# Input projection of a hybrid decoder layer in another order of groups and feature tiles, with fewer adaLN steps to a chunk

## The chip, the cores and the metric

One core of a Trainium2 chip (trn2) runs the whole layer in one launch. The metric is the device time of one execution in microseconds; three runs of the kernel before are shown, and one further execution was profiled.

## What is computed

One layer over 256 tokens of 2048 features, batch 1, all in float32:

```python
mod = silu(c) @ W_ada + b_ada                    # 2048 x 12288
shift1, scale1, gate1, shift2, scale2, gate2 = split(mod)
u = x*(1+scale1) + shift1
proj = u @ w_in                                  # 2048 x 9216: GLU 2x1024 | q | k | v | gate logits 2x2048
A = silu(LN(conv31(a_lin * sigmoid(a_gate)))) @ w_conv_out + b_conv_out
B = causal_attention(rope(q), rope(k), v) @ w_attn_out
x = LN(alpha*x + (1+gate1) * ((sigmoid(g_A)*A + sigmoid(g_B)*B) @ w_out))
u = x*(1+scale2) + shift2
x = LN(alpha*x + (1+gate2) * ((silu(conv3(a)) * val) @ w_down))     # [a | val] = u @ w_up
```

## The kernel before

Activations lie feature-major: a tile of 128 features by 256 tokens. A weight **chunk** is 128 rows by 1024 columns, 512 KB. `chunk` (L380) loads it into one of five `raw` buffers by a DMA from SP's queue, ScalarE rounds it to `wh` (L393), and VectorE takes the remainder `wl` (L394); `wh` and `wl` have three buffers each. TensorE then does wh x uh, wh x ul and wl x uh for eight blocks of 128 columns (`feat`, L401, 24 matmuls a chunk), or 12 matmuls of 512 columns for v (`toks`, L409). `uh` and `ul` are the rounded activation and its remainder.

`group` (L419) runs a row of chunks for 1024 output columns into four PSUM banks. The projection w_in has nine groups g of 1024 columns (0 and 1 the GLU input, 2 q, 3 k, 4 v, 5 to 8 the gate logits) and 16 feature tiles k, 144 chunks in all. An item (g, k0, k1) of `in_item` (L477) runs group g over feature tiles k0 to k1; a first item of a group is copied out of PSUM by ScalarE (L487), a later one is added by VectorE (L485). The list `items` (L656) sets the order.

adaLN's product with W_ada is no matmul: VectorE adds up 16 scaled row tiles for each **piece** of 1024 columns (L207; the first rows L199, L201), each from a 512 KB transfer `araw` on SP's queue, into the same `raw` buffers as the weights. A finished piece is transposed by TensorE (`pa`, L223), summed by VectorE (`red`, L225) or ScalarE (L229), and added to b_ada (`mod`, L234 and L236); `make_u` (L245) then makes `u` (L254), `uh` (L242) and `ul` (L243). The first two pieces give two feature tiles each, the next three give four each, and then come gate1, shift2 and scale2, gate2.

Three queues of background work are stepped from `chunk`: `ada_q` by rates["ada"] per chunk (a step is charged 1.15), `att_q` (rope, L576, and the attention heads) by 0.7, and `bg_q` by rates["bg"]. Into `bg_q` goes `conv` (L514), branch A's 31 taps over pairs of channel tiles: ScalarE scales a shifted tile into one of two `pr` buffers (L533) and VectorE adds it (L535, 512 columns), every sixth tap is a pair of fused operations on VectorE (L531). `conv_norm` (L538) follows: the mean by matmuls with ones (`pm`, L542) and L544, the subtraction L551, squares L552, variance `pv` (L554), L557, L558, L560, L566, silu L568 and the rounding to `chi` (L242). conv of half g starts when group g (0 or 1) is complete. w_attn_out (16 chunks) follows the projection, then w_conv_out (16), which needs `chi`, then w_out (32), w_up and w_down.

Each engine runs its instructions in one list, in order. That list isn't the order of the code: a scheduler places every instruction by an estimate of its own when the program is built.

Of the kernel before, what the change touches and what calls it, by code (L numbers as in the profile page):

```python
# [17 lines left out]
KT = D // 128  # L18
# [15 lines left out]
def layer_kernel(ctx: ExitStack, tc: tile.TileContext, x, c, w_ada, b_ada, w_in, conv_dw_w, conv_dw_b,  # L34
# [3 lines left out]
    x = x[0]  # L38
    w_ada, b_ada, w_in, w_conv_out, w_attn_out, w_out, w_up, w_down = (
        t[0] for t in (w_ada, b_ada, w_in, w_conv_out, w_attn_out, w_out, w_up, w_down))  # L40
# [12 lines left out]
    def slot(i, shape, dt, name):  # L53
        return big.tile(shape, dt, tag=f"h{i}", name=name)
# [22 lines left out]
    def wide(i, dt, name):  # L77
        return [slot(i + j, [128, 8, 256], dt, f"{name}{j}") for j in range(2)]

# [1 line left out]
    ident = cst.tile([128, 128], F32, name="ident")  # L81
    rows = slot(13, [128, 6, 128], F32, "rows")
    nc.scalar.dma_start(rows[0:16, 0], c.rearrange("o (r p) -> (o r) p", p=128))
# [49 lines left out]
        put(ropec, k_rope[0])  # L133
        put(ropes, k_rope[1])

# [1 line left out]
    xT = wide(0, F32, "xT")  # L137

    def turn_x(a, b, late=False):
# [15 lines left out]
        i = k * FT + t  # L155
        return fw[i // 88][:, i % 88:i % 88 + 1]

# [1 line left out]
    mod = cst.tile([128, 96], F32, name="mod")  # L159

    ada_done = [0]
# [214 lines left out]
    rates = {"ada": 0.0, "bg": 0.0, "att": 0.7}  # L376
    r_ada, r_bg, r_att = Rate(), Rate(), Rate()

# [1 line left out]
    def chunk(src, width, two=False):  # L380
        n = src.shape[0] // 128
        raw = st.tile([128, 1024], F32, tag="raw", name="wraw")[:, :n * width]
        if n > 1:
            nc.sync.dma_start(raw.rearrange("p (j c) -> p j c", j=n), src.rearrange("(j p) c -> p j c", j=n))
        elif two:
            nc.sync.dma_start(raw.rearrange("p (a b) -> p a b", a=2), src)
        else:
            nc.sync.dma_start(raw, src)
        if not quiet[0]:
            tick()  # L390
        wh = st.tile([128, 1024], F32R, tag="wh", name="wh", bufs=3)[:, :n * width]
        wl = st.tile([128, 1024], F32R, tag="wl", name="wl", bufs=3)[:, :n * width]
        nc.scalar.copy(wh, raw)  # L393
        nc.vector.tensor_tensor(wl, raw, wh.bitcast(F32), OP.subtract)  # L394
        if ada_done[0] < cap[0] and not quiet[0]:
            r_ada.step(ada_q, rates["ada"])
        r_att.step(att_q, rates["att"])
        r_bg.step(bg_q, rates["bg"])
        return wh, wl
# [40 lines left out]
            held = []  # L440
        return banks

# [1 line left out]
    lin = slot(6, [128, 8, 256], F32, "lin")  # L444
    gat = slot(7, [128, 8, 256], F32, "gat")
    qk = [slot(8, [128, 8, 256], F32, "q"), slot(9, [128, 8, 256], F32, "k")]
# [59 lines left out]
            elif g == 4:  # L506
                att_q.append(attention())

# [1 line left out]
    cacc, chi = [None], []  # L510

    pr = wk.tile([128, 2, 2, 256], F32, name="pr", bufs=1)
# [57 lines left out]
        yield 5.6  # L570
        quiet[0] = False

# [1 line left out]
    rps = []  # L574

    def rope(i):  # L576
# [19 lines left out]
    def attention():  # L596
# [50 lines left out]
        for i in range(4):  # L647
            cs = slice(i * 512, (i + 1) * 512)
            nc.vector.tensor_copy(flat(oh[1])[:, cs], flat(q)[:, cs])

# [1 line left out]
    ra0 = 1.0  # L652
    G0 = 4
    ra, rb = 0.35, 1.5
    items = [(g, 0, 2, 1.0, 0.0) for g in range(G0)] + [(g, 2, 4, ra0, 0.0) for g in range(G0)]
    items += [(g, 0, 4, ra0, 0.0) for g in range(G0, 9)]  # L656
    items += [(0, 4, 8, ra0, 0.0), (1, 4, 8, ra0, 0.0), (2, 4, 12, ra0, 0.0), (3, 4, 12, ra0, 0.0),
              (0, 8, KT, ra0, 0.0), (1, 8, KT, ra, rb), (2, 12, KT, ra, rb), (3, 12, KT, ra, rb)]
    items += [(g, 4, KT, ra, rb) for g in range(4, 9)]

    for _ in range(8):
        next(ada_q[0])
# [114 lines left out]
            ada_until(NB)  # L777
            drain(bg_q)

# [1 line left out]
    def norm(k, n, center):  # L781
        o = xT[k // 8][:, k % 8:k % 8 + n]
        op = nc.vector.tensor_tensor(o, o, (lc if center else la)[:, None, :].to_broadcast([128, n, 256]),
                                     OP.subtract if center else OP.mult)
        if k >= 2:
            idle(op)
# [31 lines left out]
    rest = norm_rest()  # L818
    bg_q.append(rest)

# [1 line left out]
    NP = 7  # L822
    free = [2, 3, 4, 5, 6, 7, 9, 11, 16]
    pslots, hslots = free[:NP], free[NP:] + free[:NP] + [0, 1]
# [45 lines left out]
        rates["bg"] = 0.3  # L870
    drain(bg_q)

# [1 line left out]
    lrows = [slot(i, [128, D], F32, n) for i, n in ((14, "l2g"), (15, "l2b"))]  # L874
    for r, src in zip(lrows, (ln2_g, ln2_b)):
        nc.gpsimd.dma_start(r, bass.AP(tensor=src.tensor, offset=src.offset, ap=[[0, 128], [1, D]]))
# [105 lines left out]
```

## Time and profile before

| what | value |
|---|---|
| median of three runs | 1479.33 us (1477.72 to 1479.35) |
| span of the profiled execution | 1477.4 us; its own time as a run isn't given apart |
| TensorE (PE) busy | 1417.7 us, 96% |
| VectorE (DVE) busy | 1108.8 us, 75% |
| ScalarE (ACT) busy | 796.9 us, 54% |
| DMA | 358.53 MB, mean 243 GB/s |

The span runs from the first to the last instruction; the median of the runs is 1.9 us above it. PEld is the load of a matmul's weights, which overlaps PE. A busy TensorE may still run at the lower granted clock or stand at a matmul whose end is only modelled, so busy time is read together with the count of matmuls.

### The profile page before, as it was taken

Reading aid. Unit: us, or ns where it says so; the run is one execution under the profiler, and the core shown is the slowest. Engines: PE = TensorE matmul, PEld = TensorE weight load, DVE = VectorE, ACT = ScalarE, POOL = GpSimd, SP = SyncE. Lnnn points to the kernel's source line nnn. Section 1 sums busy time; section 2 is a strip of 40 time slices with the busy share of each in tenths; the row PEclk is TensorE's granted clock in tenths of the full one; section 3 lists DMA queues with packets and bytes.
Section 4 is the critical chain, followed back from the end, with each engine's and each line's share of the span. In section 5 each row is a group of like instructions: output and inputs, shape, how many; then the busy total and the mean of one; then the engine's idle time right before and its main releaser. Section 6 shows DMA issues by size and latency. Waiting matters only on the chain.

```text
span 1477.4 us, 26835 instructions
## 1 busy us (share of the span) xinstructions
PE 1417.7 (96%) x10691; PEld 1364.2 (92%) x10691; DVE 1108.8 (75%) x1398; ACT 796.9 (54%) x1250; POOL 27.7 (2%) x57
## 2 busy tenths in 40 slices
PE   4899999999999989998999999999999999999996
PEld 4889999989999989997999999999999998888886
DVE  6788888998989879896877767988765545446456
ACT  3546436669987655345545576555444444343342
POOL 2000000210000000000000000000000000000000
PEclk9999999999999999999999999999999999999998
DMA  9999899886567657987799977778776676655662
GB/s 310 328 302 334 299 339 310 256 280 209 175 194 222 210 173 254 310 297 226 242 307 315 323 248 218 240 246 254 238 217 183 180 224 215 193 172 173 189 202 100
DMA packets 154990, 358.53 MB, mean 243 GB/s; under 512 B 12172, under 2 KB 26466, under 8 KB 154608
## 3 DMA queue, kind: packets, MB, share of 16 engines
q1 hardware_dynamic: 152704, 352.37, 74.0%
q0 software_dynamic: 1872, 4.33, 0.9%
q8 instruction: 83, 1.36, 0.4%
q14 instruction: 43, 0.35, 0.1%
q10 hardware_dynamic: 288, 0.12, 0.0%
HBM read 353.10 MB, written 2.10 MB: 240 GB/s over the span
## 4 chain that ended last, share of the span: by engine, by line
PE 75%; DMA 13%; DVE 8%; issue 2%; ACT 2%; SPq 0%; DVEq 0%; ACTq 0%
DMA araw<-in_w_ada_dram 9%; PE acc0a L405 5%; PE acc0a L407 5%; PE acc0a L406 5%; PE acc1a L405 5%; PE acc1a L407 5%; PE acc1a L406 5%; PE acc2a L406 3%; PE acc2a L407 3%; PE acc2a L405 3%; PE acc3a L405 3%; PE acc3a L406 3%; PE acc3a L407 3%; DVE wl L394 3%; DVE acc L207 2%
## 5 line engine op out<-in xcount | busy, mean ns | idle before, releaser
L393 ACT CAST wh<-wraw 128x1024 fp32r<-128x1024 f32 (+1 forms) x483 | 496.7, 1030 | 559.5 <-PE acc3a L416 132.7
L394 DVE TENSOR_TENSOR wl<-wraw,wh 128x1024 fp32r<-128x1024 f32 (+1 forms) x483 | 577.1, 1198 | 252.1 <-ACT wh L393 248.1
L207 DVE SCALAR_TENSOR_TENSOR acc<-araw,ccol,acc 128x1024 f32<-128x1024 f32 (+1 forms) x182 | 225.4, 1238 | 84.3 <-DMA araw<-in_w_ada_dram 82.6
L405 PE MATMUL acc0a<-u2h,wh 128*128 128x256 f32 x352 | 99.3, 282 | 4.8 <-ACT u2h L325 4.8
L407 PE MATMUL acc0a<-u2h,wl 128*128 128x256 f32 x352 | 100.3, 285 | 3.1 <-DVE wl L394 3.1
L405 PE MATMUL acc1a<-u2h,wh 128*128 128x256 f32 x352 | 99.4, 283 | 0.0
L406 PE MATMUL acc0a<-u2l,wh 128*128 128x256 f32 x352 | 99.4, 282 | 0.0
L406 PE MATMUL acc1a<-u2l,wh 128*128 128x256 f32 x352 | 99.2, 282 | 0.0
L407 PE MATMUL acc1a<-u2h,wl 128*128 128x256 f32 x352 | 99.2, 282 | 0.0
L533 ACT ACTIVATE pr<-hc,cw 128x256 f32<-128x256 f32 x200 | 88.8, 500 | 11.7 <-DVE cacc L535 11.3
L405 PE MATMUL acc0a<-uh,wh 128*128 128x256 f32 x256 | 74.9, 292 | 7.1 <-ACT uh L242 7.1
L407 PE MATMUL acc0a<-uh,wl 128*128 128x256 f32 x256 | 74.5, 291 | 3.2 <-DVE wl L394 3.2
L406 PE MATMUL acc0a<-ul,wh 128*128 128x256 f32 x256 | 73.4, 287 | 1.6 <-DVE ul L243 1.6
L405 PE MATMUL acc2a<-uh,wh 128*128 128x256 f32 x256 | 73.1, 286 | 0.5 <-ACT gb L487 0.5
L406 PE MATMUL acc2a<-ul,wh 128*128 128x256 f32 x256 | 73.4, 287 | 0.0
L405 PE MATMUL acc1a<-uh,wh 128*128 128x256 f32 x256 | 73.3, 286 | 0.0
L407 PE MATMUL acc1a<-uh,wl 128*128 128x256 f32 x256 | 73.2, 286 | 0.0
L407 PE MATMUL acc2a<-uh,wl 128*128 128x256 f32 x256 | 73.2, 286 | 0.0
L406 PE MATMUL acc1a<-ul,wh 128*128 128x256 f32 x256 | 73.2, 286 | 0.0
L405 PE MATMUL acc3a<-uh,wh 128*128 128x256 f32 x256 | 73.2, 286 | 0.0
L407 PE MATMUL acc3a<-uh,wl 128*128 128x256 f32 x256 | 73.0, 285 | 0.0
L406 PE MATMUL acc3a<-ul,wh 128*128 128x256 f32 x256 | 72.9, 285 | 0.0
(438 smaller groups left out, 4349.8 us busy)
## 6 DMA issues: line engine op xcount, KB each, us to landing
araw<-in_w_ada_dram SPq DMA_DIRECT2D x176, 512.0 KB, 5.1
wraw<-in_w_up_dram SPq DMA_DIRECT2D x176, 512.0 KB, 4.8
wraw<-in_w_in_dram SPq DMA_DIRECT2D x144, 512.0 KB, 4.9
wraw<-in_w_down_dram SPq DMA_DIRECT2D x55, 512.0 KB, 4.5
wraw<-in_w_down_dram SPq DMA_DIRECT2D x44, 384.0 KB, 3.7
wraw<-in_w_out_dram SPq DMA_DIRECT2D x32, 512.0 KB, 5.5
araw<-in_w_ada_dram SPq DMA_DIRECT2D x32, 256.0 KB, 5.7
wraw<-in_w_attn_out_dram SPq DMA_DIRECT2D x16, 512.0 KB, 4.5
```

Of the source, the lines that this page charges most:

```text
L207: op = nc.vector.scalar_tensor_tensor(acc, r, ccol[:, k:k + 1], acc, OP.mult, OP.add)
L393: nc.scalar.copy(wh, raw)
L394: nc.vector.tensor_tensor(wl, raw, wh.bitcast(F32), OP.subtract)
L405: nc.tensor.matmul(o, wh[:, cs], ah, start=first and i % 2 == 0, stop=False, skip_group_check=True)
L406: nc.tensor.matmul(o, wh[:, cs], al, start=False, stop=False, skip_group_check=True)
L407: nc.tensor.matmul(o, wl[:, cs], ah, start=False, stop=last, skip_group_check=True)
L533: nc.scalar.activation(pr[:, k % 2, i], src, AF.Copy, scale=w)
```

## The change

The table of items is replaced. Items (g, 0, 2) and (g, 2, 4) are now taken for five groups and not four; then four groups get tiles 4 to 8 and three groups tiles 4 to 12 ahead of the first complete group; 30 items stand where 26 stood. The rate of adaLN steps in the early items is 0.95 for the first five and 0.85 after, where it was 1.0; in the late items it is 0.42, where it was 0.35. Comment lines are emptied as well.

```diff
-    ra0 = 1.0
-    G0 = 4
-    ra, rb = 0.35, 1.5
-    items = [(g, 0, 2, 1.0, 0.0) for g in range(G0)] + [(g, 2, 4, ra0, 0.0) for g in range(G0)]
-    items += [(g, 0, 4, ra0, 0.0) for g in range(G0, 9)]
-    items += [(0, 4, 8, ra0, 0.0), (1, 4, 8, ra0, 0.0), (2, 4, 12, ra0, 0.0), (3, 4, 12, ra0, 0.0),
-              (0, 8, KT, ra0, 0.0), (1, 8, KT, ra, rb), (2, 12, KT, ra, rb), (3, 12, KT, ra, rb)]
-    items += [(g, 4, KT, ra, rb) for g in range(4, 9)]
+    ra, rb = 0.42, 1.5
+    early = [(g, 0, 2) for g in range(5)] + [(g, 2, 4) for g in range(5)] + [(g, 0, 4) for g in range(5, 9)]
+    early += [(g, 4, 8) for g in range(4)] + [(g, 4, 12) for g in range(4, 7)] + [(0, 8, KT)]
+    late = [(g, 8, KT) for g in range(1, 4)] + [(g, 12, KT) for g in range(4, 7)] + [(7, 4, KT), (8, 4, KT)]
+    items = [(*it, 0.95 if i < 5 else 0.85, 0.0) for i, it in enumerate(early)] + [(*it, ra, rb) for it in late]
```

On SP's list, counted from its start in transfers of 512 KB, adaLN stands before and now at: 15 and 14 after the eighth chunk of w_in, 41 and 37 after the 36th, 70 and 61 after the 68th, 90 and 92 after the 144th, 99 and 101 after w_conv_out, 128 and 128 after w_out; 192 and 192 at the end. The lines below the table move up by three, so L706 is now L703.

The third piece of adaLN (feature tiles 4 to 7), on TensorE's list. `pa` are the transposes of its sums, uh_94 the rounded tiles 0 to 7. Before, within the 26th chunk of the projection:

```order
L405 MATMUL acc3a<-uh_94,wh 128x256
L406 MATMUL acc3a<-ul_96,wh 128x256
L223 MATMUL pa<-ident,acc 128x128 x8
L407 MATMUL acc0a<-uh_94,wl 128x256
L405 MATMUL acc0a<-uh_94,wh 128x256
```

Now, behind the 36th chunk and ahead of the first chunk on tile 4:

```order
L405 MATMUL acc3a<-uh_94,wh 128x256
L406 MATMUL acc3a<-ul_96,wh 128x256
L407 MATMUL acc3a<-uh_94,wl 128x256
L223 MATMUL pa<-ident,acc 128x128 x4
L405 MATMUL acc0a<-uh_94,wh 128x256
L405 MATMUL acc1a<-uh_94,wh 128x256
```

The transposes stood ten chunks ahead of the first use of the new tiles, and now the second half of them stands directly ahead of it. VectorE's list behind them reads, now:

```order
L225 TENSOR_REDUCE red<-pa 128x4
L394 TENSOR_TENSOR wl<-wraw,wh 128x1024
L236 SCALAR_TENSOR_TENSOR mod<-red,bada 128x4
L207 SCALAR_TENSOR_TENSOR acc<-araw,ccol,acc 128x1024
L243 TENSOR_TENSOR ul_96<-u,uh_94 128x256 x4
```

A wl now stands between the reduction and the sum in mod.

The end of w_attn_out, on VectorE's list. cacc is the conv's sum, gb the gate of branch B, L706 (now L703) its product with the banks of w_attn_out's second group. Before:

```order
L551 TENSOR_TENSOR cacc<-cacc,pr 128x1024 x2
L394 TENSOR_TENSOR wl<-wraw,wh 128x1024
L207 SCALAR_TENSOR_TENSOR acc<-araw,ccol,acc 128x1024
L706 TENSOR_TENSOR gb_1379<-acc0a,gb_1379 128x512
L394 TENSOR_TENSOR wl<-wraw,wh 128x1024
L706 TENSOR_TENSOR gb_1379<-acc1a,gb_1379 128x512
L557 TENSOR_SCALAR pr<-pv 128x256
L706 TENSOR_TENSOR gb_1379<-acc2a,gb_1379 128x512
L560 RECIPROCAL pr<-pr 128x256
L706 TENSOR_TENSOR gb_1379<-acc3a,gb_1379 128x512
L394 TENSOR_TENSOR wl<-wraw,wh 128x1024
L566 TENSOR_TENSOR cacc<-cacc,pr 128x256 x2
```

Now:

```order
L703 TENSOR_TENSOR gb_1355<-acc3a,gb_1355 128x512
L207 SCALAR_TENSOR_TENSOR acc<-araw,ccol,acc 128x1024
L394 TENSOR_TENSOR wl<-wraw,wh 128x1024
L535 TENSOR_TENSOR cacc<-cacc,pr 128x512 x5
L531 SCALAR_TENSOR_TENSOR cacc<-hc,cw_1382,cacc 128x256 x2
L535 TENSOR_TENSOR cacc<-cacc,pr 128x512 x5
L531 SCALAR_TENSOR_TENSOR cacc<-hc,cw_1382,cacc 128x256 x2
L535 TENSOR_TENSOR cacc<-cacc,pr 128x512 x5
L531 SCALAR_TENSOR_TENSOR cacc<-hc,cw_1382,cacc 128x256 x2
L551 TENSOR_TENSOR cacc<-cacc,pr 128x1024 x2
L557 TENSOR_SCALAR pr<-pv 128x256
L560 RECIPROCAL pr<-pr 128x256
```

In both, the last wl shown is that of w_conv_out's third chunk. Fifteen tap adds and three pairs of L531 stood ahead of w_attn_out's last chunks and now stand behind that wl. On ScalarE's list the same holds of 26 instructions of L533, which now stand between the wh of that chunk and L544; behind them come five L229 ahead of L558, and no L393 until chi is made. On TensorE's list, now, with ohi the rounded attention output:

```order
L406 MATMUL acc3a<-olo,wh 128x256
L407 MATMUL acc3a<-ohi,wl 128x256
L542 MATMUL pm<-cacc,ones 128x256 x2
L554 MATMUL pv<-sq,ones 128x256 x4
L223 MATMUL pa<-ident,acc 128x128 x4
L554 MATMUL pv<-sq,ones 128x256 x4
L223 MATMUL pa<-ident,acc 128x128 x4
L405 MATMUL acc0a<-chi,wh 128x256
```

The last pm and all pv stood ahead of the last w_attn_out matmuls and now stand behind them; the eight pa stood some ten chunks later.

## Rows read from the trace of the kernel before

**Rows 1.** The page: span, and part 1 (busy time, share, instructions).
```profile
span 1477.4 us, 26835 instructions
...
PE 1417.7 (96%) x10691; PEld 1364.2 (92%) x10691; DVE 1108.8 (75%) x1398; ACT 796.9 (54%) x1250; POOL 27.7 (2%) x57
```

**Rows 2.** Waits of TensorE, 20 to 240 us: us in total, times, longest.
```profile
PE acc0a L405 <- ACT uh L242: 7.1, 3, 4.6
PE acc0a L407 <- DVE wl L394: 3.2, 4, 2.2
PE acc0a L406 <- DVE ul L243: 1.6, 1, 1.6
```

**Rows 3.** Windows: width, PE busy (matmuls), granted clock, DMA share, GB/s.
```profile
45.00:50.00 5.00, 5.00 (x44) 1.00 0.90 307
...
55.00:60.00 5.00, 4.56 (x21) 0.50 1.04 348
60.00:65.00 5.00, 5.00 (x40) 0.91 0.96 346
...
95.00:100.00 5.00, 2.78 (x22) 1.00 0.91 321
```

**Rows 4.** Timeline of TensorE about 50 us: start, us, what, idle before and releaser.
```profile
50.23 0.60 PE L223 MATMUL pa<-ident,acc 128*128 128x128 f32 x4
55.44 0.58 PE L405 MATMUL acc0a<-uh,wh 128*128 128x256 f32 x1 [4.62 <-ACT uh L242]
```

**Rows 5.** Timelines of VectorE and ScalarE in the same stretch.
```profile
51.36 0.68 DVE L225 TENSOR_REDUCE red<-pa 128x4 f32<-128x512 f32 x1
...
53.99 1.10 ACT L254 ACTIVATE u<-xT,mod 128x256 f32<-128x256 f32 x2
```

**Rows 6.** Window of all engines: PE, PEld, DVE, ACT, POOL busy, clock, DMA.
```profile
230.00:480.00 250.00, 250.00 (x1928) 243.04 (x1927) 231.16 (x332) 199.12 (x376) 15.66 (x32) 1.00 0.74 233
```

**Rows 7.** Timeline of TensorE about the end of w_attn_out.
```profile
525.68 1.24 PE L554 MATMUL pv<-sq,ones 128*128 128x256 f32 x5
...
527.59 0.28 PE L406 MATMUL acc3a<-olo,wh 128*128 128x256 f32 x1
527.71 0.28 PE L407 MATMUL acc3a<-ohi,wl 128*128 128x256 f32 x1
533.26 0.58 PE L405 MATMUL acc0a<-chi,wh 128*128 128x256 f32 x1 [5.27 <-ACT chi L242]
```

**Rows 8.** Groups by line and form: busy us, mean ns, idle before and releasers.
```profile
L394 DVE TENSOR_TENSOR wl<-wraw,wh 128x1024 fp32r<-128x1024 f32 x439 | 535.0, 1223 | 206.9 <-ACT wh L393 203.0 <-PE pg L889 1.5 <-PE acc3a L407 0.9
L207 DVE SCALAR_TENSOR_TENSOR acc<-araw,ccol,acc 128x1024 f32<-128x1024 f32 x167 | 214.2, 1282 | 82.4 <-DMA araw<-in_w_ada_dram 81.1 <-ACT acc L205 0.3 <-DVE wl L394 0.2
...
L229 ACT ACTIVATE junk<-pa 128x128 f32<-128x128 f32 x48 | 13.3, 276 | 4.1 <-PE pa L223 3.1
L229 ACT ACTIVATION_READ_ACCUMULATOR junk<-pa 128x1 f32 x48 | 9.4, 196 | 0.0
```

**Rows 9.** Timeline of ScalarE, 492 to 528 us.
```profile
492.90 1.71 ACT L533 ACTIVATE pr<-hc,cw 128x256 f32<-128x256 f32 x4
...
517.16 0.38 ACT L544 ACTIVATE pr<-pm 128x256 f32<-128x256 f32 x1 [1.13 <-PE pm L542]
...
519.67 2.04 ACT L552 ACTIVATE sq<-cacc 128x1024 f32<-128x1024 f32 x2
...
522.70 1.28 ACT L555 ACT_TABLE_LOAD   x1
...
527.55 0.42 ACT L558 ACTIVATE pr<-pr 128x256 f32<-128x256 f32 x1 [3.36 <-DVE pr L557]
```

**Rows 10.** Timeline of VectorE, 415 to 417 us.
```profile
415.03 0.87 DVE L531 SCALAR_TENSOR_TENSOR cacc<-hc,cw,cacc 128x256 f32<-128x256 f32 x2
...
416.15 1.41 DVE L535 TENSOR_TENSOR cacc<-cacc,pr 128x512 f32<-128x512 f32 x2
```

**Rows 11.** Waits of TensorE, 620 to 800 us.
```profile
PE acc0a L405 <- ACT wh L393: 2.0, 1, 2.0
```

## The prediction

> **What bounds the kernel now.** Read the page first: TensorE is busy 96% of the span [rows 1], so only its idle time and its slow clock can change the time; the question at each place is who lets it go last. The waits of TensorE over the first 240 us come next [rows 2]: 7.1 us for uh, the rounded activations, 4.6 of them in one piece; 3.2 us for wl, the weight remainders; 1.6 us for ul. Then the windows [rows 3]. At 55 to 60 us, just behind the long wait, the granted clock is 0.50, the lower of the two levels (1.2 of 2.4 GHz), and 21 matmuls ran; at 60 to 65 us 40 ran, where a full window holds 44. So the clock cost (23+4)/44 of 5 us, 3.1 us, of which 0.44 was still the wait: 2.6 us. At 95 to 100 us there is a wait of 2.2 us and the clock stays at 1.00. The DMA share there is 0.91 to 1.04 at 321 to 348 GB/s: the DMA engines are full, so a 512 KB tile costs 0.524 MB / 346 GB/s, about 1.5 us. The timeline shows what the long wait is made of [rows 4, 5]: TensorE ends its ready chunks and turns adaLN's sums at 50.23, VectorE reduces them at 51.36, ScalarE makes u at 53.99, and the next matmul starts at 55.44.
>
> From 230 to 480 us TensorE is busy all the time while VectorE is busy 231 of 250 us [rows 6]: the conv of branch A is hidden there, with little room. The next idle time is at the end of w_attn_out [rows 7]: the last matmul starts at 527.71, the first of w_conv_out at 533.26, a wait of 5.3 us for chi, the normalized conv.
>
> **The change part by part.** I count in weight chunks: 1 to 144 are w_in, 145 to 160 w_attn_out. One is 24 matmuls that start 0.12 us apart [rows 7], 2.9 us.
>
> *Opening, transfers.* Between chunks 8 and 36 SP's list has 26 adaLN transfers before and 23 now. A chunk with its share of adaLN takes (1 + 26/28) x 1.5 = 2.9 us of DMA before, TensorE's own pace, and 2.7 us now. So DMA stops being the last at these chunks. The waits behind the long one, 2.5 us for uh, 1.6 us for ul and 3.2 us for wl [rows 2], should mostly go: the fourth and fifth adaLN piece stand 4 or more chunks ahead of their use on TensorE's list, and I take half of the wl waits as gone: -5.7 us.
>
> The Trainium skill (DMA: Bandwidth & Descriptors, section Bandwidth; HBM Reference) has a core that streams alone at about 425 GB/s, so the DMA engines would have had room before and those 5.7 us would stay: 1502 in place of the forecast below. Here the share stands at 0.96 to 1.04 with 346 to 348 GB/s [rows 3], so I go by the rows.
>
> *Opening, the long wait.* Ten chunks now run before the second piece is needed, not eight, and TensorE turns its sums before the last of them. One chunk, 2.9 us, lies under the chain of 5.2 us from the turning to the first matmul [rows 4]: 2.3 us of wait are left, about the one at 97 us that kept the clock. That is 4.6 + 2.6 - 2.3 = -4.9 us. But the third piece, which before was turned ten chunks ahead of its use, is now turned directly ahead of it: TensorE's list goes from that transpose to matmuls on the new tiles. Behind it come the reduction (0.68), one wl (1.22), the add to mod, four u of 0.55 and the cast: as long as the chain of 5.2 us [rows 5, 8]. So the wait and the slow clock come again, chunk 37 in place of chunk 9: +7.2 us. Opening in all: -3.4 us. Ends: -11 if the new wait stays hidden, +2 if DMA stays last.
>
> *Middle.* The items go from 26 to 30, so 16 more adds of 512 columns on VectorE, some 11 us, and g0's projection ends at chunk 84 and not 68, so the same conv has 76 chunks and no longer 92 to hide under. VectorE had 19 us in 250 free [rows 6]; buffers of three chunks take up local excess. I charge +1 us, ends 0 and +4.
>
> *The conv's tail.* This decides. VectorE's list holds, behind the wl of w_conv_out's third chunk, 15 tap adds and 3 pairs of L531; ScalarE's holds 26 scalings behind the wh of that chunk; before, none stood there. That wh is the third ahead of TensorE and there are three buffers, so it waits for the one that TensorE frees with its last w_attn_out matmul. Both lists run in order, so all that stands behind it runs while TensorE has nothing. Worked out from that last matmul:
> - the last product with gb (about 0.7), one adaLN step (1.28) and wl (1.22) [rows 8]: 3.0 us with overlap (2.5 to 3.2);
> - the taps: two adds take 1.41 and a pair of L531 0.87 [rows 10], so VectorE alone needs 15 x 0.70 + 3 x 0.87 = 13.1 us; ScalarE needs 13 x 0.86 = 11.1 us (four scalings in 1.71 [rows 9]). They alternate over two buffers, so a little more than the longer: 14.0 (11.4 to 16);
> - from the mean to the first chi matmul: the stretch L544 to the end of L552 was 4.6 us, table load and probe 1.5, L558 to the matmul 5.7 [rows 7, 9], and ScalarE now has five adaLN sums before L558, 5 x 0.47 = 2.4 [rows 8]: 14.2. Weight copies stood inside these before and do not now: 12.0, with 0.5 for the pm matmuls (11 to 14.7).
>
> Together 29.5 us against 5.3: +24.2. TensorE's own 10 pm and pv matmuls (five of these take 1.24 [rows 7]) and 8 transposes now lie inside the wait: -3.1. The slow clock behind the wait is paid in both. Net **+21 us** (16.5 to 25.5).
>
> *w_out.* Before its last group the program asks for nine pieces at once: ten transfers in a row before, eight now, 3.0 us of DMA less. TensorE waited 2.0 us there [rows 11]: -2 us (0 to -4, if a slow clock behind the wait goes with it).
>
> The sum is 21 - 3.4 - 2 + 1 = +16.6 on the profiled execution's span of 1477.4 [rows 1]: 1494.0. The median of the runs stands 1.9 us above that span, so I forecast **1496 us**.
>
> **The rivals.**
> 1. *The opening is starved and recovers whole, and the tail is cheap: faster.* All the waits of rows 2 (11.9) and the 2.6 of clock go, w_out gives 4, taps run at VectorE's start spacing of 0.60 (15 x 0.60 + 2.6 = 11.6), the copies take 2.5 and the chain 9: 23.1 - 5.3 - 3.1 = 14.7 against 18.5, so 1475.5. It decides if the tail costs under 15.5 us net. For it: the full DMA engines. Against it: the third piece's transpose stands directly before its use. 0.06. The Trainium skill (Perfetto Trace Analysis, section Identifying the Most-Contended Engine) would lean this way, as the change feeds the engine with the highest occupancy; by its section Optimization Strategy, which wants regimes with different bounds interleaved, the conv's shorter cover speaks against it.
> 2. *The opening recovers whole, the tail as forecast*: -14.5 + 21 - 2 + 1, some 1485. 0.09; its lower part falls within no change.
> 3. *The change does not do what it says*: adaLN's transfers are 192 in both, only later, and if it was the chain and not DMA that held the opening, nothing is won there: 1501. 0.10.
> 4. *VectorE becomes the bound of the last 76 chunks*: 11 us of adds on 19 us of room, met by conv that is pressed into fewer chunks; 8 us more, 1504. For it: rows 6. Against it: adaLN's steps per chunk also move. 0.13.
>
> **How the numbers follow.** The forecast has 0.62. Range 1485 to 1507: it takes in rivals 2 to 4 and most of the tail's bounds, and leaves out rival 1 and sums of several bounds. About 0.2%, 3 us, is what a measurement of this kernel can tell from no change. Faster 0.06 (rival 1), the same 0.04 (the lower part of rival 2), slower 0.90.
>
> **What would show it.** Right: a TensorE wait for chi of 27 to 32 us, with a row of L533 and L535 and no weight copies in it; a wait of some 5 us at chunk 37 with a clock of 0.50 behind it; a wait below 3 us at chunk 11; less than 2 us before w_out's last group. Wrong: a chi wait below 20 us, or VectorE's waits (wl) of more than 3 us in all between 230 and 500 us. The forecast fails if the conv's taps are found done before w_attn_out ends.

## The result, and the profile after

The change is slower by much more than forecast: a median of 1533.18 us (1531.39 to 1536.65, four runs) beside 1479.34 us for the kernel before on the same chip, a ratio of 1.0365 with an interval of 1.0346 to 1.0383. The forecast was 1496 us, with a range that ended at 1507. The sign was right, the size was not: +54 us in place of +17.

The page of the changed kernel, span and part 1, against [rows 1]:

```profile
span 1530.9 us, 26858 instructions
...
PE 1431.3 (93%) x10691; PEld 1370.1 (89%) x10691; DVE 1119.4 (73%) x1414; ACT 800.9 (52%) x1252; POOL 27.5 (2%) x57
```

The same 10691 matmuls stand in it. TensorE is busy 13.6 us longer and idle 39.9 us longer. To see where, I take from TensorE's timeline the start of the first matmul of each stage, and subtract:

| stage on TensorE (us) | before | after | difference |
|---|---|---|---|
| start to the first w_attn_out matmul | 477.5 | 492.9 | +15.4 |
| w_attn_out, to its last matmul | 50.2 | 46.8 | -3.4 |
| from there to the first chi matmul | 5.5 | 36.2 | +30.6 |
| w_conv_out, to the first w_out matmul | 49.6 | 49.0 | -0.5 |
| w_out, to the first u2 matmul | 119.4 | 122.2 | +2.8 |
| w_up, to the first w_down matmul | 514.4 | 523.0 | +8.6 |
| first w_down matmul to the end of the span | 260.7 | 260.7 | 0 |

Half of the loss is the conv's tail (30.6 - 3.4 = 27.2 of 53.5). The projection, forecast at -2.4 us (opening and middle), lost 15.4, and w_up, which no term of the sum named, 8.6.

*Projection.* Waits of TensorE after, first 20 to 160 us (against [rows 2]), then 160 to 492 us:

```profile
PE acc0a L405 <- ACT uh L242: 13.0, 3, 7.1
PE acc0a L406 <- DVE ul L243: 1.0, 1, 1.0
```

```profile
PE s L604 <- DMA k<-rp: 2.3, 1, 2.3
PE acc0a L405 <- ACT wh L393: 2.2, 2, 1.9
PE acc0a L407 <- DVE wl L394: 1.6, 3, 0.7
PE acc2a L415 <- DVE k L485: 0.8, 1, 0.8
PE tp L624 <- ACT pp L619: 0.8, 1, 0.8
PE acc0a L417 <- DVE wl L394: 0.7, 1, 0.7
PE acc0a L415 <- ACT wh L393: 0.7, 1, 0.7
PE acc2a L405 <- DVE lin L485: 0.5, 1, 0.5
```

Windows after, with the columns of [rows 3] after the engines' (PE, PEld, DVE, ACT, POOL, then clock, DMA share, GB/s):

```profile
55.00:60.00 5.00, 1.29 (x7) 0.66 (x5) 1.96 (x2) 5.00 (x10) 0.00 (x0) 0.99 1.05 399
60.00:65.00 5.00, 4.07 (x19) 4.07 (x20) 4.52 (x6) 1.47 (x2) 0.00 (x0) 0.50 0.99 306
...
95.00:100.00 5.00, 5.00 (x44) 5.00 (x43) 4.47 (x6) 1.05 (x1) 0.00 (x0) 1.00 0.96 332
...
145.00:150.00 5.00, 0.79 (x3) 0.79 (x4) 3.85 (x7) 3.21 (x8) 0.00 (x0) 0.52 0.92 307
150.00:155.00 5.00, 5.00 (x37) 5.00 (x35) 1.90 (x3) 0.11 (x2) 0.00 (x0) 0.79 0.68 207
```

The longest wait, 7.1 us, is the one at chunk 37, with the low clock in it and behind it (0.52 and 3 matmuls from 145 to 150 us, 37 matmuls in the next 5 us where a full window holds 44). The long wait of before did not shrink: it is at chunk 11 now (3.7 us for uh and 1.0 us for ul), and the clock falls to 0.50 again. Of the waits of before the small ones for wl are gone. From 160 us on a handful of waits of 0.5 to 2.3 us, 9.6 us in all, stands where the kernel before had 2.2 us, the 1.6 us for ul of [rows 2] the longest.

What the chain ahead of chunk 11 is made of, on TensorE and ScalarE (against [rows 4, 5]):

```profile
52.18 0.60 PE L223 MATMUL pa<-ident,acc 128*128 128x128 f32 x4
59.22 0.39 PE L405 MATMUL acc0a<-uh,wh 128*128 128x256 f32 x1 [3.67 <-ACT uh L242]
```

```profile
55.38 1.09 ACT L254 ACTIVATE u<-xT,mod 128x256 f32<-128x256 f32 x2
58.74 0.73 ACT L242 CAST uh<-u 128x256 fp32r<-128x256 f32 x2
```

From the turning to the first matmul it takes 7.0 us now, before 5.2. Between u and uh ScalarE's list has three copies out of v's banks (L487) and the rounding of a weight chunk (L393); u itself stands behind the first of those copies, which waits for TensorE.

The window of [rows 6] after: VectorE has 32 us free, more than the 19 before. Under it the group of [rows 8] that changed most, L207, whose idle time before it rose from 82.4 to 111.8 us.

```profile
230.00:480.00 250.00, 242.11 (x1920) 236.49 (x1919) 217.91 (x303) 171.03 (x306) 15.70 (x32) 0.99 0.76 245
```

```profile
L207 DVE SCALAR_TENSOR_TENSOR acc<-araw,ccol,acc 128x1024 f32<-128x1024 f32 x167 | 214.3, 1283 | 111.8 <-DMA araw<-in_w_ada_dram 109.6 <-ACT acc L205 1.6
```

*Tail.* TensorE about the end of w_attn_out, against [rows 7]; then VectorE; then ScalarE; then all engines in three windows:

```profile
539.71 0.28 PE L407 MATMUL acc3a<-ohi,wl 128*128 128x256 f32 x1
559.88 2.08 PE L542 MATMUL pm<-cacc,ones 128*128 128x256 f32 x4 [19.88 <-DVE cacc L531]
564.77 3.78 PE L554 MATMUL pv<-sq,ones 128*128 128x256 f32 x8 [2.82 <-ACT sq L552]
...
568.86 1.89 PE L554 MATMUL pv<-sq,ones 128*128 128x256 f32 x8
...
575.91 0.58 PE L405 MATMUL acc0a<-chi,wh 128*128 128x256 f32 x1 [4.58 <-ACT chi L242]
```

```profile
542.80 1.28 DVE L207 SCALAR_TENSOR_TENSOR acc<-araw,ccol,acc 128x1024 f32<-128x1024 f32 x1
543.99 1.23 DVE L394 TENSOR_TENSOR wl<-wraw,wh 128x1024 fp32r<-128x1024 f32 x1
545.13 1.42 DVE L535 TENSOR_TENSOR cacc<-cacc,pr 128x512 f32<-128x512 f32 x2
546.85 1.49 DVE L535 TENSOR_TENSOR cacc<-cacc,pr 128x512 f32<-128x512 f32 x2 [0.31 <-ACT pr L533]
...
559.34 0.88 DVE L531 SCALAR_TENSOR_TENSOR cacc<-hc,cw,cacc 128x256 f32<-128x256 f32 x2
562.40 2.36 DVE L551 TENSOR_TENSOR cacc<-cacc,pr 128x1024 f32<-128x1024 f32 x2 [2.19 <-ACT pr L544]
570.79 0.42 DVE L557 TENSOR_SCALAR pr<-pv 128x256 f32<-128x256 f32 x1 [6.03 <-PE pv L554]
```

```profile
561.99 0.38 ACT L544 ACTIVATE pr<-pm 128x256 f32<-128x256 f32 x1 [3.41 <-PE pm L542]
563.66 2.19 ACT L552 ACTIVATE sq<-cacc 128x1024 f32<-128x1024 f32 x2 [1.29 <-DVE cacc L551]
565.87 1.28 ACT L555 ACT_TABLE_LOAD   x1
```

```profile
550.00:575.00 25.00, 8.64 (x28) 6.20 (x28) 14.44 (x23) 15.89 (x42) 0.00 (x0) 0.63 0.00 0
559.00:568.00 9.00, 5.30 (x12) 3.78 (x13) 3.54 (x5) 3.98 (x5) 0.00 (x0) 0.50 0.00 0
570.00:572.00 2.00, 1.34 (x8) 0.75 (x6) 0.42 (x1) 1.16 (x7) 0.00 (x0) 1.00 0.00 0
```

The chain reads as forecast, link by link: the last copies to 545.1, the row of L533 and L535 to 560.2 with no weight copy in it, then mean, variance and chi. What is new to the eye is the clock: its mean of 0.63 over the gap is 0.50 up to 568 us and 1.00 from 570 us. All pm and the first half of pv run at 0.50: a record takes 0.52 us (2.08 for 4) and 0.47 us (3.78 for 8). The second half of pv takes 0.24 us a record (1.89 for 8), as before, where five took 1.24 us [rows 7].

### The profile page after: what moved, and what is told of

The parts are those of the page before. It is cut to its first block, busy times and chain, and to the rows that moved or that the text cites. A ratio compares the mean times of both kernels' runs of the same rounds, so it can differ in the third digit from the quotient of the medians.

```text
span 1530.9 us, 26858 instructions
## 1 busy us (share of the span) xinstructions
PE 1431.3 (93%) x10691; PEld 1370.1 (89%) x10691; DVE 1119.4 (73%) x1414; ACT 800.9 (52%) x1252; POOL 27.5 (2%) x57
## 4 chain that ended last, share of the span: by engine, by line
PE 67%; DMA 15%; DVE 11%; issue 4%; ACT 3%; DVEq 0%; SPq 0%; ACTq 0%
DMA araw<-in_w_ada_dram 12%; PE acc0a L407 4%; DVE wl L394 4%; PE acc0a L405 4%; PE acc0a L406 4%; PE acc1a L407 4%; PE acc1a L405 4%; PE acc1a L406 4%; PE acc2a L407 3%; PE acc2a L405 3%; PE acc2a L406 3%; PE acc3a L407 3%; PE acc3a L406 3%; PE acc3a L405 3%; DVE acc L207 2%
## 5 line engine op out<-in xcount | busy, mean ns | idle before, releaser
L393 ACT CAST wh<-wraw 128x1024 fp32r<-128x1024 f32 (+1 forms) x483 | 496.1, 1029 | 572.9 <-PE acc3a L406 186.1
L207 DVE SCALAR_TENSOR_TENSOR acc<-araw,ccol,acc 128x1024 f32<-128x1024 f32 (+1 forms) x182 | 225.6, 1239 | 113.5 <-DMA araw<-in_w_ada_dram 111.1
L533 ACT ACTIVATE pr<-hc,cw 128x256 f32<-128x256 f32 x200 | 88.5, 500 | 21.4 <-DVE cacc L535 21.3
L407 PEld LDWEIGHTS acc0a<-u2h,wl 128*128 128x128 f32 x352 | 67.0, 190 | 11.0 <-DVE wl L394 10.8
L535 DVE TENSOR_TENSOR cacc<-cacc,pr 128x512 f32<-128x512 f32 x100 | 68.8, 688 | 6.0 <-ACT pr L533 4.4
```

The lines of the kernel that those rows point to most:

```text
L207: op = nc.vector.scalar_tensor_tensor(acc, r, ccol[:, k:k + 1], acc, OP.mult, OP.add)
L407: nc.tensor.matmul(o, wl[:, cs], ah, start=False, stop=last, skip_group_check=True)
L533: nc.scalar.activation(pr[:, k % 2, i], src, AF.Copy, scale=w)
L535: nc.vector.tensor_tensor(o, o, pr[:, k % 2], OP.add)
```

## The experiments

My theory after the result was that the loss is the tail, made by conv's late start (behind chunk 84, before 68), with smaller parts for adaLN pieces that come late. The rival was that it lies in the rates, or in any disturbance of the schedule. All lengths below are read as in the table above; ratios are to the kernel before in the same series of runs (its medians there were 1479.3 to 1483.0).

| run | to w_attn_out | wait for chi | w_up | ratio (interval) |
|---|---|---|---|---|
| before; again (e12) | 477.5; 477.4 | 5.5; 5.9 | 514.4; 515.2 | 1.0005 (0.9987 to 1.0022) |
| change | 492.9 | 36.2 | 523.0 | 1.0365 (1.0346 to 1.0383) |
| change again (e13) | 493.1 | 37.3 | 522.4 | 1.0385 (1.0351 to 1.0418) |
| e1 table only | 483.8 | 39.9 | 516.6 | 1.0291 (1.0276 to 1.0306) |
| e2 rates only | 503.1 | 20.1 | 527.0 | 1.0289 (1.0271 to 1.0308) |
| e3 conv earlier | 520.6 | 24.8 | 520.0 | 1.0429 (1.0413 to 1.0445) |
| e4 conv later | 491.7 | 36.9 | 523.6 | 1.0278 (1.0262 to 1.0293) |
| e5 last taps out | 495.3 | 24.8 | 520.8 | 1.0291 (1.0257 to 1.0326) |
| e6 fewer adaLN in w_up | 496.6 | 37.2 | 528.0 | 1.0407 (1.0373 to 1.0441) |
| e7 five groups | 477.4 | 13.3 | 523.8 | 1.0104 (1.0072 to 1.0137) |
| e8 late rate | 478.9 | 23.4 | 521.6 | 1.0151 (1.0123 to 1.0180) |
| e9 change, six buffers | 489.0 | 46.3 | 527.6 | 1.0368 (1.0321 to 1.0415) |
| e10 before, six buffers | 470.0 | 9.5 | 523.2 | 1.0020 (1.0001 to 1.0039) |
| e11 conv earlier, old rates | 505.6 | 17.6 | 529.6 | 1.0317 (1.0278 to 1.0356) |
| e14 phase of before | 495.1 | 36.4 | 518.9 | 1.0322 (1.0284 to 1.0360) |
| e15 five groups, six buffers | 470.5 | 15.8 | 516.0 | 0.9964 (0.9945 to 0.9983) |

**Table and rates apart.** e1 is the change with the rates of before:

```diff
-    ra, rb = 0.42, 1.5
+    ra, rb = 0.35, 1.5
-    items = [(*it, 0.95 if i < 5 else 0.85, 0.0) for i, it in enumerate(early)] + [(*it, ra, rb) for it in late]
+    items = [(*it, 1.0, 0.0) for i, it in enumerate(early)] + [(*it, ra, rb) for it in late]
```

> The new table of items with the adaLN rates of before (1.0 in the early items, 0.35 in the late ones). Theory (the loss sits in the conv's tail, as conv starts only behind chunk 84): the list of VectorE holds 16 tap adds and 4 pairs of L531 behind the third w_conv_out chunk, about as many as the change; the wait for chi is 33 to 40 us again; with the old early rate the third adaLN piece is turned 11 chunks ahead of its use, so the 7.1 us wait at chunk 37 is gone. Total about 1520 to 1528. Rival (the loss comes from the rates, as more adaLN is pushed into the late chunks): about 1480 to 1490, with a wait for chi under 10 us.

1523.90 us, within the theory's figure. The tail is there in full (39.9 us), the wait at chunk 37 is gone, and w_up takes 516.6 us.

e2 is the kernel before with the new rates (`ra0 = 0.85`, 0.95 in the first items, `ra, rb = 0.42, 1.5`).

> The old table with the new adaLN rates (0.95 and 0.85 early, 0.42 late). Theory: no tap stands behind the third w_conv_out chunk, so the wait for chi stays at 5 to 6 us and the time is 1474 to 1484; the loss of 8.6 us in w_up does not appear. Rival (rates carry the loss): 1500 or more. For the transfers of the opening: if DMA was what held the opening, TensorE's waits behind chunk 11 fall by 3 to 6 us; if it was the chain of adaLN, they stay.

1525.14 us: the theory fell here. No tap stands behind the third chunk of w_conv_out and still all three places lose. The projection loses 25.7 us, two waits of it at the chunks that first use the fourth and the fifth adaLN piece (TensorE's timeline):

```profile
190.89 0.58 PE L405 MATMUL acc0a<-uh,wh 128*128 128x256 f32 x1 [7.83 <-ACT uh L242]
...
250.77 0.58 PE L405 MATMUL acc0a<-uh,wh 128*128 128x256 f32 x1 [7.68 <-ACT uh L242]
```

So the table sets when a piece is due and the rate when it is done. The old table needs the rate of 1.0. In the new one, at 0.85, only the third piece is late: TensorE has no wait for uh of 0.5 us or more behind chunk 37.

e8 takes the late rate alone:

```diff
-    ra, rb = 0.35, 1.5
+    ra, rb = 0.42, 1.5
```

> The kernel before with the late adaLN rate at 0.42 and not 0.35; its early rates of 1.0 and its table stay. Theory A (in the run of the rates alone, the waits of 7.8 and 7.7 us for the fourth and fifth adaLN piece came from the early rates, the longer tail and w_up from the late rate): opening as before, tail 8 to 14 us longer, w_up 5 to 12 us longer, 1492 to 1505. Theory B (the late rate is harmless, all of it follows from the early rates' delay): 1477 to 1484.

1504.26 us, theory A: up to w_attn_out nearly as before (+1.4 us), wait for chi 17.9 us longer, w_up 7.2 longer. A rate 0.07 higher moves conv's last tap from 14.6 us ahead of the last w_attn_out matmul (513.1 against 527.7) to 6.4 us behind it (531.2 against 524.8), with the chain from the mean to chi uncovered:

```profile
530.85 2.08 PE L542 MATMUL pm<-cacc,ones 128*128 128x256 f32 x4 [5.72 <-DVE cacc L531]
536.55 3.78 PE L554 MATMUL pv<-sq,ones 128*128 128x256 f32 x8 [3.63 <-ACT sq L552]
...
548.24 0.39 PE L405 MATMUL acc0a<-chi,wh 128*128 128x256 f32 x1 [4.58 <-ACT chi L242]
```

**Conv's start moved.** e3 is the change with conv's group completed earlier:

```diff
-    early += [(g, 4, 8) for g in range(4)] + [(g, 4, 12) for g in range(4, 7)] + [(0, 8, KT)]
+    early += [(g, 4, 8) for g in range(4)] + [(0, 8, KT)] + [(g, 4, 12) for g in range(4, 7)]
```

> The changed kernel with the item (0, 8, 16) moved ahead of the three items (4 to 6, 4, 12), so that conv may start behind chunk 60 and not behind chunk 84. Theory: 3 tap adds and 1 pair of L531 are left behind the third w_conv_out chunk, so the wait for chi falls from 36 us to 12 to 18 us and the time by 18 to 25 us, to 1508 to 1515; the opening's wait at chunk 37 stays. Rival (VectorE has too much to do in the whole late part, and the tail is only where that shows): the time that the tail gives back is lost as waits for wl between 230 and 540 us, and the whole stays above 1525.

1544.67 us, slower still. The wait for chi fell, though only to 24.8 us; but the projection lost 27.7 us more, and not at wl as the rival said: the item now asks for the fifth adaLN piece 24 chunks sooner, and for the fourth 4.

```profile
213.18 0.58 PE L405 MATMUL acc0a<-uh,wh 128*128 128x256 f32 x1 [10.01 <-ACT uh L242]
...
237.96 0.58 PE L405 MATMUL acc0a<-uh,wh 128*128 128x256 f32 x1 [8.22 <-ACT uh L242]
```

e11 adds the rates of before (1.0 and 0.35) to that.

> The changed kernel with the item (0, 8, 16) moved ahead of the three items (4 to 6, 4, 12), as in the run with conv earlier, and with all adaLN rates of before (1.0 early, 0.35 late). Theory (the two losses are conv's late start and adaLN pieces that come too late for their tiles, each undone here): the fifth piece is turned three chunks ahead of its use and not directly ahead of it, so the waits for uh of 8 to 10 us are gone or below 3; no tap stands behind the third w_conv_out chunk; the wait for chi is 5 to 12 us; 1480 to 1495. Rival (the longer list of items, 30 and not 26, costs by itself through VectorE's adds): 1505 or more.

1528.81 us, outside the theory and within the rival's figure, though the longest waits are not at VectorE's adds: the fifth piece is still not done when it is due (5.8 us for its sums, then 5.7 for uh). The projection takes 505.6 us; the wait for chi falls to 17.6. In these runs conv's start is bound by the adaLN stream: at chunk 60 the pieces aren't there, at chunk 84 the taps don't fit, and before has 68. One thing is left open: e3 and e11 keep a background rate of 0.0 in the three items behind (0, 8, 16). The first scaling of a tap runs at 259.9 and 243.4 us all the same (302.8 in the change), but the early start wasn't tried with the rate of 1.5.

e4 makes the tail in the old opening:

```diff
-              (0, 8, KT, ra0, 0.0), (1, 8, KT, ra, rb), (2, 12, KT, ra, rb), (3, 12, KT, ra, rb)]
-    items += [(g, 4, KT, ra, rb) for g in range(4, 9)]
+              (2, 12, KT, ra0, 0.0), (5, 4, KT, ra0, 0.0), (0, 8, KT, ra0, 0.0), (1, 8, KT, ra, rb), (3, 12, KT, ra, rb)]
+    items += [(g, 4, KT, ra, rb) for g in (4, 6, 7, 8)]
```

> The kernel before with the items (2, 12, 16) and (5, 4, 16) moved ahead of (0, 8, 16), at rate 1.0: conv starts behind chunk 84 as in the change, and the opening, its item count of 26 and its rates are those of before. 14 tap adds and 3 pairs of L531 then stand behind the third w_conv_out chunk. Theory: a wait for chi of 33 to 37 us, and 1479 + 28 to 32 = 1507 to 1511; if the later 8.6 us of w_up follow from the tail, 1516 to 1520. Rival (the tail needs the new opening's extra adds and adaLN steps to become long): under 1495.

1521.81 us. The tail alone answers to the theory (36.9 us, 31 more than before); the time, 2 us above its second figure, less so, because (2, 12, 16) asks for the fifth piece four chunks sooner and waits 8.2 us for it. So conv's start at chunk 84 is enough for the whole tail; neither the new opening nor the late rate is needed. (The edit also keeps the adaLN rate at 1.0 for 16 chunks more.) It isn't the only way to a longer wait for chi: e2 and e8 have one of 20.1 and 23.4 us with conv's start at chunk 68.

e5 prices the taps: the last pair of channel tiles has 16 taps and not 31, so a part of branch A is not computed.

```diff
-            for k in range(CK):
-                if c0 == 6 and k == CK - 10:
+            for k in range(CK if c0 < 6 else CK - 15):
+                if c0 == 6 and k == CK - 25:
```

> The changed kernel with the last 15 of the 31 taps left out for the last pair of channel tiles of conv, so that part of branch A is not computed; everything else, the table and the rates are those of the change. Two tap adds and two scalings are left behind the third w_conv_out chunk. Theory (in the gap behind w_attn_out VectorE's taps are paid at full length): the wait for chi falls from 36.2 us by 12 to 14 us, to 22 to 24 us, and the time to 1518 to 1521; what is left of the wait is the chain from the mean to chi, about 16 us with its ten ones-matmuls at the low clock, and 5 us of copies. Rival (the chain and the copies would fill the gap anyhow, taps run beside them): above 30 us and above 1527.

The wait for chi is 24.8 us, 11.4 less, and the time 1526.15 us: both between the theory's figures and the rival's. On ScalarE an adaLN step now stands ahead of L544 and waits for its transfer:

```profile
552.31 1.15 ACT L205 ACTIVATE acc<-araw,ccol 128x1024 f32<-128x1024 f32 x1 [6.80 <-DMA araw<-in_w_ada_dram]
```

From the first pm matmul (548.95) to L544 (553.37) it takes 4.4 us where the change takes 2.1. Without those 2.3 us the taps that were left out are worth 13.7 us. VectorE's row of taps behind the last copy is 1.5 us long (547.42 to 548.90) where the change has 15.1 us, 13.6 less: they are paid at full length.

**w_up.** e6 spreads its last adaLN transfers over more chunks (rate 0.9 to 0.7 in w_up's first items).

> The changed kernel with the adaLN rate of w_up's first items at 0.7 and not 0.9, so that its last 64 transfers spread over more chunks. Theory (w_up lost 8.6 us because its first 170 us are near the limit of the DMA engines, and each late adaLN transfer holds back VectorE's next weight remainder): the stretch from the first u2 matmul to the first of w_down falls from 523.0 to 512 to 517 us, and the time to 1522 to 1528. Rival (the loss is of the clock or comes from another place): 1531 to 1536 as the change.

1540.95 us, w_up 528.0: the theory fell, and the time lies above the rival's figure too. Fewer transfers in flight with the chunks did not help. e12 and e13 are the two kernels unchanged (e12 but for a comment), profiled a second time.

> The kernel before, unchanged but for a comment, profiled a second time: how far its stages repeat from one execution to another. If the loss in w_up that nearly every run shows is of the schedule, w_up takes 513 to 517 us again (514.4 in the first profile), the wait for chi 5 to 6 us, the stretch to the first w_attn_out matmul 476 to 479. If stages scatter by themselves, w_up may take 518 to 524 us here too, with a time of 1477 to 1488.

> The changed kernel, unchanged, profiled a second time. If its stages repeat: w_in ends 13 to 17 us behind before, the wait for chi is 35 to 37 us, w_up takes 521 to 525 us, 1531 to 1537 in all. If they scatter: w_up anywhere between 514 and 528.

Stages repeat: to w_attn_out 477.4 and 493.1 us, w_up 515.2 and 522.4. Only w_out moved, by 4.7 us in the change (122.2 and 126.9). So the 7 to 9 us of w_up belong to the program. The change's median is 1539.32 us here, 6 us above its first and above the figure given for it. e14 is the change with the adaLN rate's left-over at the start of w_up set so that the transfers from there stand as before:

```diff
+    r_ada.left = -0.77
     for i, it in enumerate(fitems):
```

> The changed kernel with one line that sets the left-over of the adaLN rate to -0.77 at the start of w_up, so that from there SP's list of transfers is, one by one, that of before, and VectorE's list of adaLN steps and weight remainders too but for a few places. Theory (w_up's loss is the place of late adaLN transfers among the weight chunks): w_up falls from 523.0 to 513 to 518 us, and the time to 1524 to 1529. Rival (the place does not matter; transfers arrive at their own times and the loss is made by what the chip does): 520 to 528 us, 1530 to 1538.

1531.18 us, 8 less than the change in the same series (1539.32), though of that only 3.5 to 4 lie in w_up: 518.9 us, just outside the theory's figure, and about half of its loss. (Most of the rest lies in w_out, 120.7 us against 126.9 in e13.) The rows of w_up that show it, for each kernel TensorE's wait for wl and VectorE's group of L207 (behind the bar: busy, mean, idle before and its releaser). The change:

```profile
PE acc0a L407 <- DVE wl L394: 7.8, 11, 1.8
```

```profile
L207 DVE SCALAR_TENSOR_TENSOR acc<-araw,ccol,acc 128x1024 f32<-128x1024 f32 x62 | 79.6, 1284 | 60.8 <-DMA araw<-in_w_ada_dram 60.6
```

e14:

```profile
PE acc0a L407 <- DVE wl L394: 3.7, 4, 2.0
```

```profile
L207 DVE SCALAR_TENSOR_TENSOR acc<-araw,ccol,acc 128x1024 f32<-128x1024 f32 x62 | 79.6, 1283 | 51.4 <-DMA araw<-in_w_ada_dram 51.1
```

The kernel before:

```profile
PE acc0a L407 <- DVE wl L394: 3.1, 5, 1.0
```

```profile
L207 DVE SCALAR_TENSOR_TENSOR acc<-araw,ccol,acc 128x1024 f32<-128x1024 f32 x62 | 79.6, 1283 | 51.7 <-DMA araw<-in_w_ada_dram 51.3
```

VectorE's list runs in order: where an adaLN step stands ahead of a weight remainder that is ready, the remainder waits for the step's transfer, and TensorE for the remainder. The same steps, one chunk earlier or later, cost 4 us. Of the other half a part is TensorE's low clock. Behind e14's longest wait for wl (2.0 us) there is a window at 0.66 with 29 matmuls where a full one has 44, 1.7 us; the kernel before has none such in w_up behind its first 4 us.

```profile
802.00:807.00 5.00, 5.00 (x29) 5.00 (x30) 2.90 (x3) 2.10 (x2) 0.00 (x0) 0.66 0.92 318
```

The rest isn't settled.

**Buffers and the opening.** e9 and e10 give the change and the kernel before a sixth `raw` buffer, and two `t` buffers for four to make room.

```diff
-        raw = st.tile([128, 1024], F32, tag="raw", name="wraw")[:, :n * width]
+        raw = st.tile([128, 1024], F32, tag="raw", name="wraw", bufs=6)[:, :n * width]
-                raw = st.tile([128, 1024], F32, tag="raw", name="araw")
+                raw = st.tile([128, 1024], F32, tag="raw", name="araw", bufs=6)
```

(and `tag="t", bufs=4` becomes `bufs=2` in its four places.)

> The changed kernel with six raw buffers for weight chunks and adaLN transfers where five stood (four small t buffers become two to make room). Theory (w_up loses because VectorE's list puts an adaLN step, whose transfer is late for want of a free raw buffer, ahead of a weight remainder that is ready): VectorE's idle time ahead of L207 in w_up falls from 44 us by more than 10, w_up from 523.0 to 508 to 516 us; the tail stays, as as many taps stand behind the third w_conv_out chunk; 1515 to 1526 in all. Rival (DMA engines are simply full there): w_up stays at 520 us or more, 1530 or more.

> The kernel before with the same six raw buffers and two t buffers. Theory (buffers decide): w_up falls by 2 to 4 us from 514.4, the opening by 2 to 5 us; 1470 to 1477. Rival (its DMA engines are full in the opening, and it has little idle time in w_up to win): 1477 to 1484; two t buffers could cost 1 to 3 us where u2 is made.

e9: 1537.67 us, e10: 1485.18. The theory fell in both: w_up grows, to 527.6 and 523.2 us, in e10 with a list of transfers that is the same as before's, one by one. The same waits grow with it: VectorE's idle time ahead of L207 there is 82.4 and 76.1 us, TensorE's wait for wl 11.2 and 6.5. (The two t buffers alone don't make w_up longer: e15 has them too, and takes 516.0.) e9's tail grew as well, to 46.3 us, with 17 adds and four pairs of L531 behind w_conv_out's third chunk. But the opening won more than expected: e10 reaches w_attn_out 7.5 us sooner. All engines, 25 to 200 us, first before and then e10:

```profile
25.00:200.00 175.00, 164.81 (x1274) 160.45 (x1273) 144.69 (x158) 89.25 (x126) 0.00 (x0) 0.98 0.92 315
```

```profile
25.00:200.00 175.00, 171.48 (x1350) 168.89 (x1351) 152.46 (x166) 93.84 (x131) 0.00 (x0) 0.98 0.95 335
```

The DMA engines had another 20 GB/s to give, and a sixth buffer was enough to get it. 76 matmuls more ran in the same time.

e7 changes one number of the kernel before (`G0 = 4` to 5), e15 that and the six buffers.

> The kernel before with one number changed: the opening takes five groups and not four over feature tiles 0 to 2 and 2 to 4; rates and the rest of the table stay, so conv starts behind chunk 68. Theory (the change's loss is made of the late start of conv and of the late rate): no tap behind the third w_conv_out chunk; wait for chi 5 to 8 us; the opening about even with before, as in the run with the table alone; 1476 to 1486. Rival (any shift of the list costs, as the schedule of before sits in a narrow optimum): 1490 or more, with w_up 5 us or more longer.

> The kernel before with five groups in the opening and six raw buffers (two t buffers). From the runs with each alone: five groups left the opening even and its waits were for weights (wh, wl), six buffers won 7.5 us up to the first w_attn_out matmul, by having the weights there earlier. Theory (they add up): the first w_attn_out matmul 8 to 13 us earlier than before, wait for chi 9 to 14 us, w_up 515 to 525 us, 1472 to 1485 in all: the one of these versions that may beat before. Rival (the sixth buffer lets transfers run ahead only once): opening at -4 to -8 us, 1483 to 1492.

e7: 1495.86 us, with its opening even (477.4), a longer wait for chi (13.3) and a longer w_up (523.8): the rival's figures. e15: 1475.27 us, 0.36% faster than before (interval 0.17 to 0.55%) and the only version here that beats both kernels. Its time is the theory's, but the two edits don't add up: at w_attn_out it is 7.0 us ahead, no more than six buffers alone (7.5) and the rival's figure; w_up is at 516.0, and the wait for chi, 15.8, is above the theory's. Its profiled execution was with 1479.72 us the second slowest of its ten, and in that one the tail gives the 7 us back; so where the median's 6 us stay isn't shown.

## Why the prediction was right and wrong

Forecast and measured, in the terms of the sum (us): opening -3.4 and +3.4, middle +1 and +12.0, tail +21 and +27.2, w_out -2 and +2.8; the stages that it has no term for, w_up +8.6 and w_conv_out -0.5. That is +16.6 against +53.5 on the span. Opening and middle part where TensorE starts its 43rd chunk (164.4 us before, 167.8 after).

- **The tail, right in mechanism, mis-sized in its terms.** Every link was there. From the last w_attn_out matmul to the first with chi it measured 36.2 us against 29.5 worked out: copies 5.4 and not 3.0 (VectorE entered the gap with two weight remainders, two products with gb, a pair of L531 and one adaLN step still ahead of the row of taps); taps 15.1 and not 14.0; from the last tap to chi 15.7 and not 12.5. In that last term I gave pm 0.5 us and pv nothing beyond ScalarE's table load. In the gap pm and half of pv run at a clock of 0.50: pm takes 2 us, and VectorE idles 6.0 us for pv. "The slow clock behind the wait is paid in both" was true, but not inside it. With w_attn_out's -3.4 us the net is +27.2 against +21. e4 shows that the cause which was predicted, conv's start, is enough alone.
- **The opening, wrong.** By chunk 36 I had 10.6 us won; TensorE's last matmul of it starts 2.6 us earlier than before (141.37 against 144.01). The step that failed is "2.3 us of wait are left". One chunk did lie under the chain, but the chain took 7.0 us and not 5.2, as ScalarE's list has copies of v's banks between u and uh: 3.7 us were left for uh and 1.0 for ul, and the clock fell to 0.50 again, so the 4.9 us did not come. The new wait at chunk 37 came where forecast and cost about what was forecast, some 8 us against 7.2, but by luck of two errors: the wait was 7.1 us and not 4.6, from a chain of 7.7 us (141.49 to 149.21) and not 5.2, and the slow clock behind it took about 1 us and not 2.6.
- **What held the opening.** I took the DMA engines as full, from shares of 0.96 to 1.04 at 346 to 348 GB/s [rows 3]. That reading was wrong: after, one window moved 399 GB/s at a share of 1.05, and e10, with one more buffer and the same list of transfers, won 7.5 us with more bytes in the same stretch. The Trainium skill (DMA: Bandwidth & Descriptors, section Bandwidth), weighed there with its 425 GB/s for a core that streams alone, spoke for room, and by that rule fewer transfers win nothing. The windows agree that there was room, up to the 399 GB/s seen; no run here shows 425. For the opening rival 3, nothing won there, was the nearest and had 0.10; no rival came near the whole. (Its 1501 doesn't come out of its own words: the sum without the -3.4 gives 1499.)
- **The middle, wrong: +1 forecast, +12.0 measured** behind chunk 42. Some 7 of them are the waits from 160 us on that the result shows, 9.6 against 2.2 us; the clock falls once behind two of them. VectorE is not the bound (rival 4): TensorE's waits for wl there are small, 2.3 us, and VectorE has more room than before. No one cause is shown: the table alone costs 6.4 us up to w_attn_out (e1), the late rate alone 1.4 (e8), the two rates 25.7 with the old table (e2), and what the early rates do with the new table wasn't tried alone.
- **w_out, wrong in sign:** -2 forecast, +2.8 and, in the second profile, +7.5. The wait for wh of [rows 11] did shrink from 2.0 to 0.6 us, but others came (2.1 us at pms, a sum by matmuls with ones in the layer norm, for sq).
- **w_up, missing.** The sum put it at nothing without a reason: a stage that isn't edited was taken to last as long as before. Its code is the same, but the left-over of a rate shifts each adaLN step against the chunks: 8.6 us, of which e14 shows about half.
- **The range** took in the ends of the named terms, and 0 for what the change only shifts. The middle, w_out and w_up all went the same way, 23 us together.

## What to carry to other kernels

A table that sets when data is due and a rate that sets when it is done are one setting: moving either alone cost 2.9% here (e1, e2). In a kernel whose engines run long ordered lists that a scheduler fills, a shift in one stage can re-deal the stages behind it; add such a term to the range, and profile an unchanged kernel twice to learn how much of a stage's length is the program's. And before DMA is called full, try one more buffer: alone it won 7.5 us in the opening here, lost again later, and with one more group in the opening it was the only edit that made the kernel faster, by 0.36%.

## What was not expected of the hardware

The DMA share of a window reached 1.04 to 1.05 both at 348 and at 399 GB/s, so a share near 1 did not mean that no more could be moved. Matmuls in float32 with a matrix of ones, 0.25 us a record in a busy stretch, take 0.47 to 0.52 in the part of a gap where the granted clock is 0.50, and there they are links of the chain. Two executions of one program differ by less than 1 us at w_attn_out's start and in w_up, while edits far ahead of w_up move it by up to 15 us.
